# Two attentions on one core: the transposes of a group alternate with products of the matrix fill instead of standing in a row

## Chip, cores and metric

The kernel runs on one core of one Trainium2 chip. The metric is device time in microseconds (us) of one execution, the median of the runs shown. A profiled execution of its own gives the span and the trace.

## The reference, cut to what matters

Two transformer blocks run over 1024 tokens of width 1024, in float32. Each block has an attention, and each attention needs transposes of its weights of attention:

```python
# block 1: sliding window, 8 heads, blocks of 128 queries, 256 keys each
scores = einsum('bnqhgd,bnkhd->bnhgqk', qb, keys) * scale      # masked to the band
probs = softmax(concat([scores, sink]))[..., :-1]
out = einsum('bnhgqk,bnkhd->bnqhgd', probs, vals)
# block 2: stick breaking, 8 heads, blocks of 128 queries, all earlier keys
z = einsum('bhqd,bhkd->bhqk', qb, k) * scale
between = cumsum(log_sigmoid(-z), reverse) - log_sigmoid(-z)
out = einsum('bhqk,bhkd->bhqd', exp(log_sigmoid(z) + between), v)
# block 2: differential, 4 heads
out = (softmax(q1 @ k1.T) - lam * softmax(q2 @ k2.T)) @ v
```

Around them stand projections of 1024 x 1024 tokens by some thousand columns each. Those of w_in, w_in_2 and w_gate_2 bear on the change.

## The kernel before, in words

Every float32 product is made of three TensorE matmuls of rounded halves (high by high, high by low, low by high), each with a 128x128 weight and 512 moving columns. One such matmul is called a product below, and a run of 24 of them fills one accumulation bank.

Two classes carry the order of the work. `Fill` (line 115) is a generator of projections: each step of `run` (line 134) issues one product at line 152, calls `tick`, which runs the callbacks that are due (evacuations of a finished bank four products after its last one, stores, later parts of a norm), calls `units.ahead()`, which may issue the rounding of the next weight unit (high half at line 101, low half at line 102) and the load of the one two further on, and yields. `Plan` (line 163) holds the attention's steps by tick and slot. `Plan.run` (line 172) writes out by hand the order of TensorE (PE), ScalarE (ACT), VectorE (DVE) and GpSimd (POOL): in every tick it goes through the slots; at a slot with a name it issues the steps put there, at a slot with a number it draws products from the fill until `due(t, slot)` have been given in all. The count is cumulative, so that what was given early is not given again.

In **block 1** (`attention`, line 799) a tile of 128 queries has two groups of heads with one or two key blocks: 30 groups of four transposes in all. In a tick the slots are A, B, B2, 0, E, D0, D, F, C, F2, 1, G, H. `turn` (line 849, slot D) issues the group's four transposes at line 852 into a bank called `tp`; `halves` (slot F, line 857) copies it on ACT, `low` (slot F2, line 861) subtracts on DVE, and `pv` (slot D0 of the next tick, lines 265 to 267) multiplies the result with the values. Slot 1 lies after F2.

In **block 2** the slots are load, A, A2, B, B2, C0, C, 0, D0, D, F, 1, G. There are 96 units of stick breaking (12 a head) and 48 units of the differential attention, each with one to four key blocks of 128, and so one to four transposes, made by `transposed` (line 1732, the transposes at line 1735). For a stick unit the scores are in slot B (lines 1723 to 1729), `weigh` in slot A of the next tick (ACT lines 1813 to 1815, DVE lines 1816 to 1825), `final` in A2 (line 1828), the transposes (`mid`) in slot G, the last of tick t+2, the split of their bank (`end`, lines 296 and 297) in slot C of t+3 and `pv` (line 1836) in slot D0 of t+4. For a differential unit the transposes are in slot D, `end` in slot F of the same tick, and `pv` (line 1976) in slot G of the next. Eight more groups of four turn the finished differential output (line 1921). The last user of `transposed` is `diff_qk` (line 1676): 16 groups of four, called by the fill's own callbacks.

There are two `tp` banks, two `mm` banks for the fill, three `sc` banks for scores and one `po` bank. SyncE (SP) issues the loads and stores, in the order in which the program comes to them.

Of the kernel before, what the change touches and what calls it, by code (L numbers as in the profile page):

```python
# [114 lines left out]
class Fill:  # L115
# [18 lines left out]
    def run(self):  # L134

        kern, units = self.kern, self.units
        for kind, half, tt, us, free, out in self.products:
            ps = kern.ps("mm")
            ah, al = kern.actH[half], kern.actL[half]
            for k in range(KT):  # L140
                if kind == "n":
                    wh, wl = (w[:, k * P : k * P + P] for w in units.get(us[0]))
                    xh, xl = ah[:, k, :], al[:, k, :]
                    steps = ((wh, xh), (wh, xl), (wl, xh))
                else:
                    c = slice((k % 2) * HALF, (k % 2) * HALF + HALF)
                    wh, wl = (w[:, c] for w in units.get(us[k // 2]))
                    s = slice(tt * P, tt * P + P)
                    xh, xl = ah[:, k, s], al[:, k, s]
                    steps = ((xh, wh), (xh, wl), (xl, wh))  # L150
                for i, (l, r) in enumerate(steps):
                    kern.last_mm = kern.nc.tensor.matmul(ps, l, r, start=k == 0 and i == 0, stop=k == KT - 1 and i == 2)  # L152
                    self.tick()
                    if i == 2 and free and (k == KT - 1 if kind == "n" else k % 2 == 1):
                        self.after(6 if kind == "t" else 2, units.free)
                    units.ahead()
                    yield
            self.after(LAG, lambda out=out, ps=ps: out(ps))
        while self.late:
            self.tick()  # L160


class Plan:
# [8 lines left out]
    def run(self, ticks, slots, fill, due, lead=0):  # L172

        E = mybir.EngineType
        steps = fill.run()
        given = 0
        with self.tc.manual_schedule(engines={E.PE, E.Activation, E.DVE, E.Pool}):
            for t in range(ticks):
                while given < lead:
                    next(steps, None)  # L180
                    given += 1
                for slot in slots:
                    if isinstance(slot, int):
                        while given < due(t, slot):
                            next(steps, None)
                            given += 1
                    else:
                        for fn in self.ev.pop((t, slot), ()):
                            fn()
            for _ in steps:  # L190
                pass
        assert not self.ev and not fill.late, (self.ev, fill.late)


class Kern:
# [311 lines left out]
    def block1_mix(self, stack):  # L507
# [287 lines left out]
        plan = Plan(self.tc)  # L795
# [3 lines left out]
        def attention(t):  # L799
# [49 lines left out]
            def turn(g, b):  # L849
                pt = A["pt"] = self.ps("tp")  # L850
                for j in range(4):
                    nc.tensor.transpose(pt[:, j * P : j * P + P], A[g * 4 + j][:, b * P : b * P + P], self.ident)

            def halves(g, b):
                h = self.t(pl, [P, HALF], "pth", bufs=2, dt=F32R)
                A["hl"] = h, self.t(pl, [P, HALF], "ptl", bufs=2, dt=F32R)
                nc.scalar.copy(h, A["pt"])
# [38 lines left out]
            for g in range(2):  # L896
                for b in range(nb):
                    u = t0 + 5 + g * 2 + b
                    at(u, "D", lambda g=g, b=b: turn(g, b))
                    at(u, "F", lambda g=g, b=b: halves(g, b))  # L900
                    at(u, "F2", low)
                    at(u + 1, "D0", lambda g=g, b=b: pv(g, b))
                at(u + 1, "F", lambda g=g: out(g))
# [67 lines left out]
        for t in range(NT):  # L971
            attention(t)
# [624 lines left out]
    def block2_attn(self, stack):  # L1597
# [45 lines left out]
        def diff_qk(which):  # L1643
# [31 lines left out]
            def turn(t, qn):  # L1675
                pt = transposed(qn.rearrange("p h d -> p (h d)"), 4)
                fill[0].after(3, lambda: store(t, pt))
# [54 lines left out]
        def transposed(src, nb):  # L1732
            pt = self.ps("tp")
            for i in range(nb):
                nc.tensor.transpose(pt[:, i * P : i * P + P], src[:, i * P : i * P + P], self.ident)  # L1735
            return pt

        def cut(L):
# [9 lines left out]
        plan = Plan(self.tc)  # L1748
# [3 lines left out]
        def paired(d, key, w):  # L1752


            def mid():
                d["pt"] = transposed(d[key], w // P)

            def end():
                hl = d["hl"] = self.t(pl, [P, 4, 2, P], "phl", bufs=3, dt=F32R)[:, : w // P]
                self.split(hl[:, :, 0, :], hl[:, :, 1, :], d["pt"][:, :w].rearrange("p (a b) -> p a b", b=P))  # L1760

            return mid, end
# [117 lines left out]
        def diff_tile(H, h, qt, chunks, L):  # L1880
# [39 lines left out]
            def turn():  # L1920
                Q["pt"] = transposed(Q["o4"].rearrange("p a b -> p (a b)"), 4)
# [94 lines left out]
        n = len(ticks)  # L2016
# [332 lines left out]
```

## Time and profile before

| what | us |
|---|---|
| median of the runs shown | 2677.01 (2676.76 to 2686.59) |
| profiled execution, its own time | 2672.5 |
| its span, first to last instruction | 2670.7 |
| PE busy | 2597.1 (97% of the span) |
| weight loads of PE (PEld) busy | 2085.7 (78%) |
| DVE, ACT, POOL busy | 1870.3, 1158.2, 660.9 (70%, 43%, 25%) |

The first attention with its fill lies at 113 to 345 us of the span, the second at 1129 to 1830 us. PE's matmuls are pipelined and their ends are modelled, so durations overlap: what an instruction costs on PE is read from the distance between starts, not from its duration. PEld rows are the loads of the 128x128 weights that stand before each matmul. A number in square brackets behind a row is idle time of that engine before it, with what ended it.

### The profile page before, as it was taken

How to read it: one execution, taken by the hardware profiler on the slowest of the kernel's cores; microseconds unless marked ns; L12 is line 12 of the kernel's file. 1: busy time of each engine (PE TensorE's matmuls, PEld its weight loads, DVE VectorE, ACT ScalarE, POOL GpSimd, SP SyncE). 2: the span in 40 equal slices, each digit the busy share in tenths (PEclk: the TensorE clock that was granted, in tenths of full speed). 3: DMA queues.
4: the chain of work that ended last, by engine and by line, in shares of the span. 5: the costliest groups of instructions: out<-in, count | busy, mean ns of one | idle time of the engine just before them, and what ended most of it. 6: DMA issues, size and time to landing. Idle time of an engine off the chain costs nothing. (4 is left out here: it accounts for less than half of the span.)

```text
span 2670.7 us, 34280 instructions
## 1 busy us (share of the span) xinstructions
PE 2597.1 (97%) x12078; PEld 2085.7 (78%) x12078; DVE 1870.3 (70%) x2836; ACT 1158.2 (43%) x2080; POOL 660.9 (25%) x571
## 2 busy tenths in 40 slices
PE   9999999999999999899999999999999999999999
PEld 8766787788778778677777777787887788887887
DVE  5688867887887566726788777775636767776654
ACT  3444525433333334526766765554316222323442
POOL 4323254002343332311255111110001003331501
PEclk8999999999999999999999999999999999999999
DMA  6243575434555886346344343336634446565973
GB/s 257 80 158 123 162 264 193 175 137 169 200 171 192 301 285 216 126 128 198 92 131 126 123 132 116 112 105 230 240 142 144 158 140 209 171 215 189 369 243 133
DMA packets 224604, 470.84 MB, mean 176 GB/s; under 512 B 26672, under 2 KB 73904, under 8 KB 224432
## 3 DMA queue, kind: packets, MB, share of 16 engines
q1 hardware_dynamic: 224432, 468.65, 52.3%
q8 instruction: 95, 1.56, 0.2%
q14 instruction: 77, 0.63, 0.1%
HBM read 331.18 MB, written 137.36 MB: 175 GB/s over the span
## 5 line engine op out<-in xcount | busy, mean ns | idle before, releaser
L1353 POOL TENSOR_TENSOR raw<-raw,raw 128x512 f32<-128x512 f32 x78 | 141.3, 1811 | 417.0 <-DMA raw<-in_w_down 210.8
L152 PE MATMUL mm<-ah,wh 128*128 128x512 f32 x544 | 219.8, 404 | 1.8 <-DVE gb L606 1.8
L152 PE MATMUL mm<-ah,wl 128*128 128x512 f32 x544 | 219.3, 403 | 0.0
L152 PE MATMUL mm<-al,wh 128*128 128x512 f32 x544 | 219.0, 403 | 0.0
L102 POOL TENSOR_TENSOR wl<-raw,wh 128x1024 fp32r<-128x1024 f32 x44 | 106.5, 2421 | 399.3 <-DVE wh L101 159.8
L1216 DVE TENSOR_TENSOR W<-W 128x1024 f32<-128x1024 f32 x132 | 129.9, 987 | 14.5 <-DMA W<-in_w_up 12.5
L152 PEld LDWEIGHTS mm<-ah,wh 128*128 128x128 f32 x544 | 102.6, 189 | 22.5 <-issue 2.6
L152 PEld LDWEIGHTS mm<-ah,wl 128*128 128x128 f32 x544 | 102.6, 189 | 20.7 <-issue 2.5
L152 PEld LDWEIGHTS mm<-al,wh 128*128 128x128 f32 x544 | 102.7, 189 | 20.1 <-issue 2.2
L152 PE MATMUL mm<-wl,ah 128*128 128x512 f32 x256 | 102.4, 400 | 1.0 <-DVE wl L102 0.8
L152 PE MATMUL mm<-wh,al 128*128 128x512 f32 x256 | 103.2, 403 | 0.0
L152 PE MATMUL mm<-wh,ah 128*128 128x512 f32 x256 | 102.3, 400 | 0.0
L1152 PE MATMUL sc<-s,wh 128*128 128x512 f32 x344 | 100.6, 394 | 1.6 <-DVE u L1288 1.5
L1820 DVE TENSOR_TENSOR_SCAN w<-sc,w,w 128x383 f32<-128x383 f32 (+3 forms) x96 | 97.4, 1015 | 3.4
L297 DVE TENSOR_TENSOR wl<-rb,wh 128x1024 fp32r<-128x1024 f32 x52 | 77.1, 1483 | 23.7 <-ACT wh L296 19.4
L1507 PE MATMUL sc<-wh,ah 128*128 128x512 f32 x272 | 91.2, 389 | 0.0
L297 DVE TENSOR_TENSOR phl<-tp,phl 128x512 fp32r<-128x512 f32 (+2 forms) x144 | 78.3, 544 | 15.6 <-ACT phl L296 15.5
L1152 PE MATMUL mm<-ah,wh 128*128 128x512 f32 x236 | 79.7, 400 | 8.8 <-DVE wt L1105 5.0
L1816 DVE SCALAR_TENSOR_TENSOR w<-sc,w 128x384 f32<-128x384 f32 (+3 forms) x96 | 53.2, 554 | 45.7 <-ACT w L1815 45.4
L296 ACT CAST phl<-tp 128x512 fp32r<-128x512 f32 (+2 forms) x144 | 67.9, 472 | 34.5 <-PE tp L1735 34.2
L244 POOL TENSOR_SCALAR rs<-ss 128x1 f32<-128x1 f32 x40 | 16.5, 413 | 264.4 <-ACT xn L312 243.3
L1152 PE MATMUL mm<-al,wh 128*128 128x512 f32 x236 | 77.9, 399 | 3.9 <-ACT s L1172 3.9
(561 smaller groups left out, 7603.9 us busy)
## 6 DMA issues: line engine op xcount, KB each, us to landing
W<-in_w_up SPq DMA_DIRECT2D x88, 512.0 KB, 4.5
adaw<-in_ada_w SPq DMA_DIRECT2D x64, 256.0 KB, 3.0
raw<-in_w_in SPq DMA_DIRECT2D x31, 512.0 KB, 3.7
Fa<-g SPq DMA_DIRECT2D x44, 256.0 KB, 2.6
Fb<-g SPq DMA_DIRECT2D x44, 256.0 KB, 2.9
tw<-in_w_down SPq DMA_DIRECT2D x20, 512.0 KB, 5.3
rb<-in_w_down SPq DMA_DIRECT2D x40, 256.0 KB, 5.3
raw<-Fa SPq DMA_DIRECT2D x18, 512.0 KB, 4.9
```

Source lines behind the costliest of these rows:

```text
L102: (nc.vector if i in self.vec else nc.gpsimd).tensor_tensor(out=wl, in0=raw, in1=wh.bitcast(F32), op=ALU.subtract)
L152: kern.last_mm = kern.nc.tensor.matmul(ps, l, r, start=k == 0 and i == 0, stop=k == KT - 1 and i == 2)
L244: self.nc.gpsimd.tensor_scalar(out=out, in0=ss, scalar1=1.0 / n, scalar2=EPS, op0=ALU.mult, op1=ALU.add)
L296: nc.scalar.copy(h, src)
L297: nc.vector.tensor_tensor(out=l, in0=src, in1=h.bitcast(F32), op=ALU.subtract)
L1152: self.last_mm = nc.tensor.matmul(ps, l, r, start=first and k == 0 and i == 0, stop=last and k == 3 and i == 2, skip_group_check=True)
L1216: sub = lambda out, x, y: nc.vector.tensor_tensor(out=out, in0=x, in1=y, op=ALU.subtract)
L1353: eng.tensor_tensor(out=q[out], in0=q[x], in1=q[y], op=op)
L1507: self.last_mm = nc.tensor.matmul(bank, l, r, start=opens and i == 0 and j == 0, stop=closes and i == n - 1 and j == 2, skip_group_check=True)
L1816: nc.vector.scalar_tensor_tensor(out=ls, in0=z, scalar=0.0, in1=ls, op0=ALU.min, op1=ALU.subtract)
L1820: nc.vector.tensor_tensor_scan(out=sg[:, : w - 1][:, ::-1], data0=z[:, 1:w][:, ::-1], data1=ls[:, : w - 1][:, ::-1], initial=sg[:, w - 1 : ...
```

## The change

After every transpose of `turn` and `transposed` a new function of the plan, `one`, draws one product from the fill. It does so only when the plan's lead has been given and when the fill is not running already, so that a group issued from one of the fill's callbacks draws nothing. The product counts as given. The loops that draw up to a number become `more(n)`, which sets and clears the flag.

```diff
         given = 0
+        running = False
+
+        def one():
+
+            nonlocal given, running
+            if given >= lead and not running:
+                running = True
+                next(steps, None)
+                running = False
+                given += 1
+
+        def more(n):
+            nonlocal given, running
+            running = True
+            while given < n:
+                next(steps, None)
+                given += 1
+            running = False
+
+        self.one = one
...
-                while given < lead:
-                    next(steps, None)
-                    given += 1
+                more(lead)
                 for slot in slots:
                     if isinstance(slot, int):
-                        while given < due(t, slot):
-                            next(steps, None)
-                            given += 1
+                        more(due(t, slot))
...
                     nc.tensor.transpose(pt[:, j * P : j * P + P], A[g * 4 + j][:, b * P : b * P + P], self.ident)
+                    plan.one()
...
                 nc.tensor.transpose(pt[:, i * P : i * P + P], src[:, i * P : i * P + P], self.ident)
+                plan.one()
```

## Rows read from the trace of the kernel before

**Rows 1.** Windows of both attentions: busy us (x instructions) PE, PEld, DVE, ACT, POOL; clock; DMA.
```profile
113.00:345.00 232.00, 221.70 (x1123) 165.58 (x1122) 183.69 (x432) 108.55 (x254) 68.01 (x51) 0.99 0.49 155
1129.00:1830.00 701.00, 687.82 (x3486) 538.54 (x3485) 497.95 (x1052) 403.96 (x976) 156.49 (x187) 1.00 0.42 126
```

**Rows 2.** Groups of PE, both attentions: count | busy us, mean ns | idle before, releaser.
```profile
L1735 PE MATMUL tp<-cons,w 128*128 128x128 f32 x432 | 70.8, 273 | 3.5 <-DVE phl L297 3.5
...
L1735 PE MATMUL tp<-cons,do 128*128 128x128 f32 x32 | 4.8, 272 | 0.0
...
L852 PE MATMUL tp<-cons,prob 128*128 128x128 f32 x120 | 18.6, 276 | 0.2 <-DVE prob L847 0.2
```

**Rows 3.** Timeline of PE, a group of four: start us, us, engine, line, tiles, count.
```profile
1643.38 0.39 PE L152 MATMUL mm<-al,wh 128*128 128x512 f32 x1
1643.61 0.60 PE L1735 MATMUL tp<-cons,w 128*128 128x128 f32 x4
...
1644.29 0.39 PE L152 MATMUL mm<-ah,wh 128*128 128x512 f32 x1
```

**Rows 4.** Timeline of PE and PEld, a transpose alone between products.
```profile
1649.07 0.39 PE L152 MATMUL mm<-ah,wl 128*128 128x512 f32 x1
1649.30 0.27 PE L1735 MATMUL tp<-cons,w 128*128 128x128 f32 x1
...
1649.64 0.40 PE L152 MATMUL mm<-al,wh 128*128 128x512 f32 x1
...
1650.10 0.39 PE L152 MATMUL mm<-ah,wh 128*128 128x512 f32 x1
...
1649.30 0.19 PEld L152 LDWEIGHTS mm<-ah,wh 128*128 128x128 f32 x1
```

**Rows 5.** Timeline of PE, eight matmuls of one column each.
```profile
230.85 0.95 PE L379 MATMUL tp<-cons,ada 128*128 128x1 f32 x8
231.66 0.43 PE L265 MATMUL po<-pth,vh 128*64 128x512 f32 x1
```

**Rows 6.** Timeline of PE around equal scores: behind a product, behind two transposes.
```profile
1156.81 0.40 PE L152 MATMUL mm<-wl,ah 128*128 128x512 f32 x1
...
1157.73 0.45 PE L152 MATMUL mm<-wh,al 128*128 128x512 f32 x1
...
1216.49 0.39 PE L152 MATMUL mm<-ah,wh 128*128 128x512 f32 x1
...
1217.63 0.45 PE L152 MATMUL mm<-al,wh 128*128 128x512 f32 x1
```

**Rows 7.** Timeline of a group of block 1 and its readers.
```profile
309.93 0.63 PE L852 MATMUL tp<-cons,prob 128*128 128x128 f32 x4
...
311.21 0.69 DVE L861 TENSOR_TENSOR ptl<-tp,pth 128x512 fp32r<-128x512 f32 x1 [0.95 <-ACT pth L857]
...
313.63 0.40 PE L266 MATMUL po<-ptl,vh 128*64 128x512 f32 x1
```

**Rows 8.** Timeline of a stick unit, from its scores to its transposes.
```profile
1284.29 0.33 PE L1729 MATMUL sc<-r_stm,r_ident 128*128 128x128 f32 x1
...
1284.76 0.60 ACT L1813 ACTIVATE w<-sc 128x512 f32<-128x512 f32 x1
...
1286.59 0.62 ACT L1828 ACTIVATE w<-w 128x512 f32<-128x512 f32 x1
...
1287.62 0.49 PE L1735 MATMUL tp<-cons,w 128*128 128x128 f32 x3
```

**Rows 9.** Groups of DVE, block 1: part of an evacuation of the fill.
```profile
L603 DVE SCALAR_TENSOR_TENSOR gb<-u,cols,gb 128x512 f32<-128x512 f32 x12 | 10.6, 884 | 1.3 <-ACT gb L601 1.0
```

**Rows 10.** Waits of PE in both attentions: us in total, times, longest us.
```profile
PE tp L1735 <- DVE phl L297: 3.5, 4, 1.4
PE po L1836 <- DVE phl L297: 2.1, 2, 1.6
...
PE po L266 <- DVE ptl L861: 3.3, 5, 1.3
```

## Prediction

> **What bounds the kernel now.** I first read the windows over the two attentions [rows 1]. PE is busy for 221.7 of 232 us in the first and 687.8 of 701 us in the second, at a granted clock of 0.99 and 1.00 of full speed, that is the upper of its two levels, 2.4 GHz. Next come DVE with 184 of 232 and 498 of 701 us. So PE sets the time of both stretches, and all that the change can win or lose is PE time: what a transpose costs, and the 10.3 + 13.2 = 23.5 us in which PE has nothing to run.
>
> Then I counted [rows 2]: 432 transposes for the weights of attention in block 2, 32 for the differential output, 120 in block 1, together 584. By the code they stand in 144 + 8 + 30 = 182 groups. The change puts a product between neighbours at 584 - 182 = 402 places. The product drawn behind a group's last transpose stands where the next work of PE stood before. Durations are of no use here, since matmuls overlap (273 ns a transpose by its mean); the distances of starts in the timeline of PE are.
>
> A group of four [rows 3]: from the product at 1643.38 to the one at 1644.29 lie 0.91 us, which hold two products and four transposes. A transpose alone [rows 4]: from 1649.07 to 1649.64 lie 0.57 us with two products and one transpose; the next two products take 1650.10 - 1649.64 = 0.46 us, 0.23 each. So four in a row cost 0.91 - 0.46 = 0.45 us, 0.11 each, and one between two products costs 0.57 - 0.46 = 0.11 us. That is the reading on which the prediction rests: **the price is the same in both places.**
>
> Why it should be so is seen from two rows. Eight matmuls of a single moving column each need 231.66 - 230.85 = 0.81 us [rows 5], 0.10 apiece, so between short matmuls it is the next weight load that sets the pace, not the columns. And behind the lone transpose the load of the product's weights starts at 1649.30, with the transpose's own start [rows 4], and not earlier: it can't hide in the product before, because there the transpose's load stands. In a row each transpose waits for its own load, and at the end the product waits for its load: four exposed loads for four transposes. Alternating, each transpose's load hides behind a product, and each product's load behind a transpose of 0.11 us is exposed instead: four again.
>
> **The change, part by part.**
>
> *402 places where a product now separates two transposes.* One switch to a transpose and back costs 0.11 us with the transpose itself in it [rows 4], as does each in a row [rows 3]. 402 x (0.11 - 0.11) = 0 us. No row shows two such switches within one product's time, so the price is bounded from both sides. Below, the transpose could vanish behind the products: -0.11 us each, 402 x 0.11 = -44 us. Above, the product's load could be laid bare in full, 0.19 us [rows 4] in place of 0.11: 402 x 0.08 = +32 us. I take 0, since rows 4 hold both switches and are the nearest by far: nothing in an alternation differs from them but what stands two matmuls away.
>
> The Trainium skill, TensorE: Matmul & The Clock Gate (Back-to-back issue gap), gives 134 cycles for a matmul of 128 columns at the full clock, 56 ns as an estimate. By that figure a transpose whose load is hidden would cost 0.056 instead of 0.11 us and the sum would be 402 x 0.054 = 22 us lower; the lone transpose of rows 4 has its load hidden and costs 0.11, so the trace disagrees.
>
> *The product behind a group's last transpose.* In 96 stick units the next work of PE is the scores of slot B. The same scores of 256 columns take from product to product 1157.73 - 1156.81 = 0.92 us behind a product and 1217.63 - 1216.49 = 1.14 us behind two transposes [rows 6]: a difference of 0.22, twice 0.11. So what follows a group does not matter either: 0 us.
>
> *What the products take with them.* Each drawn product runs the callbacks that are due. These move earlier by up to four products in the order of ACT, DVE and POOL, and the stores and weight loads among them pass up to one tick's loads of queries and keys in SP's order. No work is added. The count is cumulative, so the slot behind draws as many fewer, and the fill ends with the same number of products. POOL is busy for 157 of 701 us [rows 1] and has room. What SP loads is wanted some ticks later: I cost it at nothing, and where that cover fails, PE waits for weights or queries at a transfer's lateness. Weight by weight, the load, its rounding and its product keep their order.
>
> *What gets late.* A group of four now takes three products longer: its last transpose comes 3 x 0.23 = 0.69 us later, and so does the copy by ACT and the subtraction by DVE where these wait for it. In block 1 a group's low half is ready at 311.21 + 0.69 = 311.90 and the matmul that reads it starts at 313.63 [rows 7], 1.7 us later. Of this 0.69 goes: covered, and 1.0 us is left. But an evacuation that now stands ahead of `low` can take this too: two of the multiplications of a convolution alone are 2 x 0.884 = 1.77 us of DVE [rows 9]. Of the 624 products of the first fill (26 outputs of 24) 120 are drawn in groups, 19%, so some 5 of 26 evacuations move ahead of their group's split; each may overrun the slack by 0.69 + 1.77 - 1.7, up to 0.8 us, and I take 0.4 us: +2 us. In block 2 the fill has 74 outputs and the distance from a group to `pv` is a whole tick or more. In the second place the scores of a stick unit come up to four products (0.92 us) later against its own transposes. In the tightest unit that I found the scores' last matmul starts at 1284.29, ACT reads them at 1284.76, its last exponential ends at 1286.59 + 0.62 = 1287.21 and the transposes follow at 1287.62 [rows 8]: 0.41 us to spare. Here the group between is of three, so the scores come 0.69 later; ACT had 0.1 us of margin behind them, the chain slips by 0.6 and the transposes wait 0.2 us. It is the tightest that I found; I count such slips at under 0.5 us in all, and let them go into the rounding.
>
> The waits for a late split are now 3.5 + 2.1 + 3.3 = 8.9 us [rows 10]. Below: all of them vanish by a luckier order, -9 us. Above: each of block 1's 30 groups loses 0.5 us, the middle between nothing and a bit over the 0.8 above, +15 us.
>
> **Sum.** 0 + 0 + 2 us on the profiled execution of 2672.5 gives 2674.5. The median of the runs is 4.5 us above that execution, so the forecast is 2679 us, 0.1% from the median. About 0.5%, 13 us, is what a measurement of this kernel can tell from no change.
>
> **Rivals.**
>
> *The loads hide (faster).* If PE loaded two weights ahead, a transpose between products would cost less than in a row. With all of it hidden the time is 2679 - 44 = 2635 us, with half of it 2657. (By the Trainium skill's figure, quoted above, the half is what would come.) For it speaks that the load of a transpose indeed begins with the product before [rows 3, 4]; against it that the lone transpose has this already and still costs 0.11 us. Chance 0.05.
>
> *Alternating lays the product's load bare (slower).* The place is the first matmul behind each inner transpose, the price 0.19 - 0.11 = 0.08 us, and it decides from the second switch on, when the next load must wait until the transpose's weights have been left. 402 x 0.08 = 32 us, 2711 us. The rows for a lone transpose show no such loss over two products, but none shows the pair repeated. Chance 0.05.
>
> *The split comes too late (slower).* The cover of `pv` and of the stick chain is used up, by the 0.69 us together with evacuations that moved forward. It decides when some 20 groups lose 0.7 us each, 14 us: 2693 us. For it: DVE has 48 us of room in 232 in block 1 and the waits of rows 10 show groups with no slack; against it: where ACT or DVE is the late one already, a later transpose changes nothing, and most groups keep over 1 us. Chance 0.05, of which 0.04 lies beyond 0.5%.
>
> *The change does nothing.* If the guard kept `one` from drawing, or the fill had run out, the order would be the old one: 2677 us. The guard does so for the 16 groups that come from the fill's callbacks, no others, and the products reach to the end of the attention. It is inside the forecast's range.
>
> **How the numbers follow.** The forecast (with the last rival in it) has 0.85. Faster by over 0.5%: 0.05. Slower by over 0.5%: 0.05 + 0.04 = 0.09. Within: 0.86. The range takes in the bounds of the stalls against the 2677 us of now, -9 and +15 us: 2668 to 2692 us. It leaves the two rivals of the loads outside, with 1 in 10 between them.
>
> **What the next profile would show.** Right: in the timeline of PE a transpose and a product alternate with 0.34 us from transpose to transpose (0.23 + 0.11), 1.36 us for four pairs, against 0.45 + 0.92 = 1.37 before; the busy time of DVE and ACT is the same; idle time of PE over both attentions is 20 to 30 us. Wrong: pairs at 0.29 us or less (the loads hide), at 0.42 us (they are laid bare), or PE waits of over 15 us more at lines 266, 1836 and 1976, or a granted clock under 0.99 in a stretch of groups. Should the scores of stick units show idle time of ACT in front of line 1813 that grows by more than 0.9 us a unit, the term for what gets late is too small.

## The result, and the profile after

The changed kernel takes 2698.31 us (median of 7 runs, 2690.65 to 2704.49) against 2679.70 us before in the same comparison: a ratio of 1.0059, 95% interval 1.0044 to 1.0075. The medians lie 18.6 us apart; the ratio is not the quotient of the medians and stands for some 16 us. No measurable change was forecast, and the time lies 6 us above the range. The profiled execution took 2700.85 us, its span is 2699.1 us.

The windows over both attentions, each from the first to the last product of its fill (columns as in [rows 1]), first of the kernel before, cut the same way:

```profile
113.50:343.30 229.80, 219.50 (x1113) 163.74 (x1112) 181.85 (x429) 106.80 (x252) 65.81 (x51) 0.99 0.48 154
1129.10:1824.70 695.60, 682.42 (x3463) 534.12 (x3462) 495.11 (x1049) 399.44 (x970) 156.49 (x187) 1.00 0.41 125
```

and of the changed kernel:

```profile
117.10:355.50 238.40, 221.75 (x1113) 162.14 (x1112) 183.32 (x429) 107.11 (x252) 65.85 (x51) 0.99 0.46 147
1145.80:1851.30 705.50, 690.04 (x3462) 525.28 (x3461) 494.82 (x1049) 401.98 (x970) 159.02 (x187) 0.99 0.41 123
```

The instructions are the same. The first attention is 8.6 us longer, and PE idles for 238.40 - 221.75 = 16.6 us of it instead of 10.3. The second is 9.9 us longer, with 15.5 us idle instead of 13.2 and a lower clock, so that PE's busy time grew too. The other 10 us of the spans' difference lie ahead of, between and behind the attentions, where nothing was edited. I don't explain them: over the profiles of this study these stretches take 112.3 to 117.1, 784.3 to 790.3 and 843.3 to 850.5 us, in no order with the edits. That the two attentions alone (18.5 us) make about the 18.6 us between the medians is chance: against a second profile of the kernel before (the control below) they are 13.1 us longer, 10.6 us of it idle time of PE.

The alternation itself is as forecast. PE's timeline in the changed kernel, a group of four (columns as in [rows 3], which it answers to):

```profile
1669.85 0.27 PE L1752 MATMUL tp<-cons,w 128*128 128x128 f32 x1
1669.88 0.48 PE L152 MATMUL mm<-ah,wl 128*128 128x512 f32 x1
1670.19 0.27 PE L1752 MATMUL tp<-cons,w 128*128 128x128 f32 x1
1670.22 0.48 PE L152 MATMUL mm<-ah,wh 128*128 128x512 f32 x1
1670.54 0.27 PE L1752 MATMUL tp<-cons,w 128*128 128x128 f32 x1
```

From transpose to transpose lie 0.34 and 0.35 us, 0.23 for the product and 0.11 to 0.12 for the transpose, the price in a row. The starts of a pair differ by 0.03 us only, but the sum of the two is what it was.

What grew are waits. PE's waits in the changed kernel, first attention and then second (line, total us, times, longest us; compare [rows 10]; lines 282, 1752 and 1854 were 266, 1735 and 1836):

```profile
PE po L282 <- DVE ptl L878: 6.6, 7, 1.5
PE po L281 <- ACT pth L874: 3.1, 2, 2.0
...
PE tp L1752 <- DVE phl L313: 7.6, 5, 3.8
...
PE po L1854 <- DVE phl L313: 1.2, 2, 0.7
```

Line 282 waits for the low half of block 1's weights 6.6 instead of 3.3 us, line 281 for the high half 3.1 instead of 0.6 us, and transposes in block 2 wait for a free bank, that is for the split at line 313, 7.6 instead of 3.5 us. Of the 7.6, one wait of 3.79 us is that of `diff_qk`'s transposes, which did not wait before; the transposes of the weights wait 3.8 us, about as long as before.

**The largest stall of the first attention.** The changed kernel's timeline from a group's last transpose to its value products:

```profile
300.62 0.27 PE L868 MATMUL tp<-cons,prob 128*128 128x128 f32 x1
...
302.58 0.71 ACT L617 ACTIVATE gb<-u,cols 128x512 f32<-128x512 f32 x1
303.33 1.54 DVE L619 SCALAR_TENSOR_TENSOR gb<-u,cols,gb 128x512 f32<-128x512 f32 x2 [1.43 <-ACT gb L617]
304.90 0.75 DVE L622 SCALAR_TENSOR_TENSOR gb<-mm,cols,gb 128x512 f32<-128x512 f32 x1
305.69 0.63 ACT L626 ACTIVATE gb<-gb 128x512 f32<-128x512 f32 x1 [2.40 <-DVE gb L622]
305.97 2.15 DVE L863 TENSOR_SCALAR prob<-prob,den 128x256 f32<-128x256 f32 x4
306.23 0.57 ACT L874 CAST pth<-tp 128x512 fp32r<-128x512 f32 x1
306.85 0.45 PE L281 MATMUL po<-pth,vh 128*64 128x512 f32 x1 [2.02 <-ACT pth L874]
308.05 0.68 DVE L878 TENSOR_TENSOR ptl<-tp,pth 128x512 fp32r<-128x512 f32 x1
308.78 0.69 PE L282 MATMUL po<-ptl,vh 128*64 128x512 f32 x1 [1.49 <-DVE ptl L878]
```

The transposes are done at 301, but ACT copies the bank (line 874) only at 306.23. ACT first has exponentials until 302.58. Then comes, still ahead of the copy, a convolution's finish, which goes from ACT to DVE and back to ACT (lines 617 to 626): ACT idles for 2.40 us inside it, though the copy behind had all that it needed. The Trainium skill, PSUM — Partial Sum Buffer (Engine vs sequencer instructions), says that the queues of ScalarE and VectorE are strict first-in first-out; the row at 305.69 agrees. The second wait, 1.49 us, has DVE ahead of it: the scaling of attention weights (line 863, slot C) starts only behind the finish, at 305.97, and takes 2.15 us, where the kernel before takes 1.14; why it is slower here is not shown. In the kernel before the same finish of the same place comes behind the copy (then line 857), and PE waits for nothing:

```profile
294.82 0.56 ACT L857 CAST pth<-tp 128x512 fp32r<-128x512 f32 x1
295.29 0.72 ACT L601 ACTIVATE gb<-u,cols 128x512 f32<-128x512 f32 x1
...
296.82 0.68 DVE L861 TENSOR_TENSOR ptl<-tp,pth 128x512 fp32r<-128x512 f32 x1
297.42 1.53 DVE L603 SCALAR_TENSOR_TENSOR gb<-u,cols,gb 128x512 f32<-128x512 f32 x2
298.49 0.39 PE L266 MATMUL po<-ptl,vh 128*64 128x512 f32 x1
```

**The largest stall of the second attention.** The changed kernel's timeline:

```profile
1480.78 0.69 DVE L101 CAST wh<-raw 128x1024 fp32r<-128x1024 f32 x1 [1.82 <-DMA raw<-in_w_in2t]
1481.51 1.23 DVE L102 TENSOR_TENSOR wl<-raw,wh 128x1024 fp32r<-128x1024 f32 x1
...
1484.75 0.40 DVE L313 TENSOR_TENSOR phl<-tp,phl 128x256 fp32r<-128x256 f32 x1
1485.21 1.12 PE L1752 MATMUL tp<-cons,dqn 128*128 128x128 f32 x4 [3.79 <-DVE phl L313]
```

DVE waits 1.82 us for the load of a weight unit, with its rounding (lines 101, 102) at the head of the queue; behind the rounding comes the next unit's scan (lines 1834 to 1838, 1482.65 to 1484.84), and only then the split that frees a bank of transposes. PE stands for 3.79 us. This is the largest wait, but by the experiments below the loss does not come and go with it.

With both stalls the granted clock falls. Windows of the changed kernel (columns as in [rows 1]), up to the first stall and behind it, and from inside the second (PE idles until 1485.21):

```profile
301.00:307.00 6.00, 3.98 (x19) 2.31 (x17) 4.43 (x11) 3.60 (x12) 0.60 (x1) 1.00 0.57 179
308.00:314.50 6.50, 5.72 (x19) 3.80 (x20) 4.49 (x15) 2.46 (x7) 1.11 (x2) 0.50 0.14 40
...
1482.00:1488.50 6.50, 3.29 (x10) 2.32 (x11) 5.54 (x11) 1.11 (x2) 4.75 (x7) 0.50 0.77 267
```

0.50 is the lower level, 1.2 GHz. PE runs at half speed where it has work again, and so a stall costs more than its idle time.

### The profile page after: what moved, and what is told of

Same layout as the page of the kernel before. It is cut to its first block, busy times and chain, and to the rows that moved or that the text cites. A ratio compares the mean times of both kernels' runs of the same rounds, so it can differ in the third digit from the quotient of the medians.

```text
span 2699.1 us, 34278 instructions
## 1 busy us (share of the span) xinstructions
PE 2615.1 (97%) x12078; PEld 2082.0 (77%) x12078; DVE 1875.0 (69%) x2836; ACT 1161.3 (43%) x2080; POOL 656.9 (24%) x571
## 5 line engine op out<-in xcount | busy, mean ns | idle before, releaser
L152 PE MATMUL mm<-ah,wh 128*128 128x512 f32 x544 | 229.2, 421 | 2.3 <-DVE gb L622 2.3
L152 PE MATMUL mm<-ah,wl 128*128 128x512 f32 x544 | 229.0, 421 | 0.0
L152 PE MATMUL mm<-al,wh 128*128 128x512 f32 x544 | 228.9, 421 | 0.0
L1752 PE MATMUL tp<-cons,w 128*128 128x128 f32 x432 | 117.6, 272 | 3.8 <-DVE phl L313 3.8
L152 PE MATMUL mm<-wl,ah 128*128 128x512 f32 x256 | 108.4, 424 | 2.1 <-POOL wl L102 2.1
L152 PE MATMUL mm<-wh,al 128*128 128x512 f32 x256 | 109.2, 427 | 0.0
L152 PE MATMUL mm<-wh,ah 128*128 128x512 f32 x256 | 108.2, 423 | 0.0
L1169 PE MATMUL mm<-ah,wh 128*128 128x512 f32 x236 | 80.0, 402 | 9.7 <-DVE wt L1122 6.0
L1169 PE MATMUL mm<-al,wh 128*128 128x512 f32 x236 | 78.1, 400 | 3.8 <-ACT s L1189 3.8
```

The lines of the kernel that those rows point to most:

```text
L1169: self.last_mm = nc.tensor.matmul(ps, l, r, start=first and k == 0 and i == 0, stop=last and k == 3 and i == 2, skip_group_check=True)
```

## Experiments

Ratios are against the kernel before, run beside each kernel on the same chip.

**The two attentions apart.** The first keeps `plan.one()` in `turn` alone, the second in `transposed` alone.

```diff
 # first only: in transposed
-                plan.one()
 # second only: in turn
-                    plan.one()
```

> Alternation in the first attention only (30 groups). Theory, order and bank: the change costs PE stalls in both attentions, because the drawn products carry their evacuations and weight roundings ahead of the group's own split, and because the last transpose is late; then this run keeps the 8.7 us that the first attention lost in the profile and none of the second's 9.9: 2686 to 2690 us, first attention 238 us long, second 696. Rival, the clock alone (a general loss of granted clock by the alternating stream): the first attention's share is 90 of 402 places, 4 us, 2684 us, with no more idle time of PE than before.

> Alternation in the second attention only (152 groups). Theory: first attention at 230 us as before, second at 703 to 706, 2688 to 2692 us, with waits of PE at the transposes on the split of the group before (line 1752) and drops of the granted clock behind them. Rival, chance: the second attention's loss was three drops of the clock that fall by luck; then its length comes back to 696 to 699 us and the time to 2680 to 2684.

First only: 2690.20 us, 1.0032 (1.0019 to 1.0045). Second only: 2688.02 us, 1.0026 (1.0011 to 1.0041). 0.32% + 0.26% = 0.58%, as much as the whole change in its first comparison (0.59%; its repeat below gave 0.40%). Windows of the edited attention, first of the one and then of the other kernel:

```profile
116.80:355.20 238.40, 221.79 (x1113) 162.19 (x1112) 183.26 (x429) 107.07 (x252) 65.79 (x51) 0.99 0.44 146
```

```profile
1131.10:1836.40 705.30, 690.04 (x3463) 525.39 (x3461) 494.59 (x1049) 401.70 (x970) 158.76 (x187) 0.99 0.40 123
```

They repeat the lengths and idle times of the changed kernel to 0.3 us. Each attention pays for itself. By length alone one profile would not show this: the second attention, unedited, took 699.2 us in the kernel with the first only, and 704.0 us in the one with the subtraction moved in the first attention (below), against 695.6 us in the first profile of before. Its idle time keeps the two apart: 11.3 to 13.2 us in every profile with that attention unedited, 14.3 to 16.7 us in every one with the alternation and its callbacks.

**The transposes in a row again, the products directly behind them.** This leaves the early draw and takes the alternation away.

```diff
                 for j in range(4):
                     nc.tensor.transpose(pt[:, j * P : j * P + P], A[g * 4 + j][:, b * P : b * P + P], self.ident)
+                for j in range(4):
                     plan.one()
...
                 nc.tensor.transpose(pt[:, i * P : i * P + P], src[:, i * P : i * P + P], self.ident)
+            for i in range(nb):
                 plan.one()
```

> Both attentions; the transposes of a group stand in a row as before, and the same number of products is drawn directly behind the group's last one. So the callbacks of the products move as in the changed kernel, the last transpose is as early as before. Theory, moved callbacks: as slow as the changed kernel, 2694 to 2702 us, idle time of PE in the first attention near 16 us. Rival, the late last transpose: back to 2680 us, first attention 230 us.

2688.01 us, 1.0029 (1.0016 to 1.0042): half of the loss or more stays with no alternation in it; the time lies between the two expectations. Its windows:

```profile
114.40:346.90 232.50, 221.59 (x1112) 164.81 (x1111) 181.75 (x429) 106.98 (x252) 65.28 (x51) 0.99 0.45 152
1132.90:1836.90 704.00, 688.54 (x3462) 531.72 (x3461) 495.11 (x1049) 400.19 (x970) 157.92 (x187) 0.99 0.40 124
```

PE's idle time falls to 10.9 us in the first attention, and stays at 15.5 in the second.

**The alternation without what products call.** Drawn products run no callbacks and no roundings; what is owed is paid with the next product of a numbered slot.

```diff
+    def pay(self):
+        while self.owed and not self.quiet:
+            self.owed -= 1
+            self.tick()
+            self.units.ahead()
...
-                    self.tick()
+                    self.owed += 1
+                    self.pay()
...
-                    units.ahead()
+                    if not self.quiet:
+                        units.ahead()
...
-                running = True
+                running = fill.quiet = True
```

> The changed kernel, but a product drawn in a group runs no callbacks and rounds no weights; they are run behind the next product that is drawn outside a group. The transposes alternate and the last one is late as in the change, the callbacks stand behind the group's split, as before. Theory, moved callbacks: 2680 to 2684 us. Rival, the late last transpose: 2694 to 2700 us.

2687.83 us, 1.0024 (1.0010 to 1.0038). Better than the change, but no return to before: PE idles for 12.5 us in the first attention and 13.9 in the second. It lies between what was expected of either theory. By the code, what is owed is paid in one burst, roundings and the freeing of units among it, and the last transpose is still late; which of these keeps the loss is not told apart by this run.

**The changed kernel again, and whose wait it is.** In block 2 the wait of 3.8 us is that of `diff_qk`'s own transposes (rows above: `dqn`) for a bank, so one theory was that too many groups want the two banks. The second kernel lets no such group come out of a drawn product.

```diff
-        for x in [x for x in self.late if x[0] <= self.clock]:
+        for x in [x for x in self.late if x[0] <= self.clock and not (self.quiet and x[1] in self.held)]:
...
-                fill[0].after(TURN_LAG, lambda: turn(t, qn))
+                later = lambda: turn(t, qn)
+                fill[0].held.add(later)
+                fill[0].after(TURN_LAG, later)
```

> The changed kernel once more, beside the others and on their chip. If the two attentions add up (e1 +0.32%, e2 +0.26%): +0.5 to +0.65%, 2694 to 2699 us; its profile with the same lengths of the two attentions as before, 238 and 705 us, within 3 us. If they don't add, 2688 to 2692.

> The changed kernel, but the fill's own transposes (16 groups of the query and key norms) are not issued between or directly behind the transposes of a group of the plan: when they fall due in a group they wait for the next product outside of one. Theory, two transpose banks: the wait of 3.8 us at the fill's transposes on the split of the group before goes down to under 1.5 us, the second attention from 705 to 701 us or less, its idle time from 15.5 to 11 to 13 us, time 3 to 6 us under the changed kernel. Rival, DVE's backlog whatever the bank: the wait moves to the next reader of the split, the length stays at 704 to 706.

Again: 2693.55 us, 1.0040 (1.0021 to 1.0058). Its profile has the first attention at 238.0 us with 14.6 us idle and the second at 705.3 us with 15.4. Turn held out: 2693.41 us, 1.0044 (1.0030 to 1.0057), the same. PE's groups of instructions in its second attention (columns as in [rows 2]):

```profile
L1755 PE MATMUL tp<-cons,w 128*128 128x128 f32 x432 | 118.0, 273 | 3.8 <-DVE phl L314 3.8
L1755 PE MATMUL tp<-cons,dqn 128*128 128x128 f32 x64 | 10.1, 282 | 2.6 <-DVE phl L314 2.6
```

The wait did not move to another user of the bank: `diff_qk`'s transposes (`dqn`) still stand, 2.6 us instead of 3.8, and those of the weights wait 3.8 us as in the change. Neither the fall to under 1.5 us that the theory asked for nor the move that its rival expected came, and the second attention is no shorter (706.1 us). So keeping these groups out of drawn products does not mend it; what PE waits for is still DVE's split.

**The subtraction ahead of slot C in block 1**, in the kernel before and in the changed one. If the place of `low` in DVE's order were the cause, this would mend it.

```diff
-... "F", "C", "F2", 1, "G", "H")
+... "F", "F2", "C", 1, "G", "H")
```

> The kernel before with one edit: in the first attention the split's subtraction (slot F2) is issued on DVE ahead of the scaling of the weights (slot C). Theory, a late split is what stalls PE at the value matmuls: their 4.4 us of waits fall to 1 to 2 us, the first attention from 230 to 225 to 227 us, time 2674 to 2678. Rival, DVE's throughput: what is moved back delays the transposes in their turn, the length stays within 1 us.

> The changed kernel with the same one edit. Theory: its waits at the value matmuls (9.7 us in the profile) fall by 4 to 6 us, the first attention from 238 to 232 to 234 us, the time 4 to 7 us under the changed kernel. Where an evacuation holds ACT in front of the split's copy the wait stays, so not all goes. Rival as in the run without the change: within 1 us of 238.

On the kernel before 2686.06 us, 1.0011 (0.9998 to 1.0025); on the changed one 2701.65 us, 1.0058 (1.0039 to 1.0077), no better than the change itself. PE's waits in the first attention of the former:

```profile
PE sc L815 <- DVE rm L823: 3.1, 3, 1.7
PE sc L815 <- DVE ql L300: 1.7, 1, 1.7
...
PE po L266 <- DVE ptl L861: 0.6, 2, 0.3
```

The wait of line 266 shrank from 3.3 to 0.6 us, and scores wait for DVE at line 815 instead; the idle time of the first attention is 11.0 us, against 10.3 before. `low` is not wrongly placed by itself; here moving one part of DVE's work handed the wait to the next. In the changed kernel the first attention took 243.5 us, with 15.7 us idle at a clock of 0.96.

**Callbacks or roundings, with a control.** The control is the kernel before once more. One kernel takes only the roundings out of the drawn products, the other only the callbacks (but those that free a weight unit).

```diff
 # roundings out: where a product of the fill is issued
-                    units.ahead()
+                    if not self.quiet:
+                        units.ahead()
 # callbacks out: in tick
-        for x in [x for x in self.late if x[0] <= self.clock]:
+        for x in [x for x in self.late if x[0] <= self.clock and (not self.quiet or x[1] == self.units.free)]:
...
 # both: in one
-                running = True
+                running = fill.quiet = True
```

> The kernel before, once more, for a second profile of it. If its first profile (granted clock 0.999 in the second attention) was a lucky one, as the lengths of the unchanged second attention in other runs say (699 and 704 us): first attention 228 to 233 us, second 697 to 704 us at a clock of 0.984 to 0.995, with the same 13 us of idle time of PE. Rival, the first profile is typical: second attention 694 to 697 us, clock 0.997 or more.

> The changed kernel, but a product drawn in a group does not call for the rounding of the next weight unit; its other callbacks run as in the change. Theory for the second attention: a rounding that waits on DVE for its load stands ahead of the next unit's scan and split; without it the wait of 3.8 us goes, idle time of PE there from 15.5 to 13 or 14 us, length 698 to 702 us; the first attention stays at 237 to 239 us; time 2685 to 2691. Rival, the evacuations: the second attention stays at 15 us idle and 704 to 706 us, time 2692 to 2697.

> The complement: a product drawn in a group calls for roundings as in the change, but runs no other callbacks (evacuations, later parts of norms, the fill's own transposes) than the freeing of a unit. Theory: the first attention, whose evacuations of a convolution hold ACT and DVE ahead of the split, goes from 238 to 232 to 235 us with 11 to 13 us idle; the second keeps its waits, 15 us idle, 702 to 706 us; time 2687 to 2692. Rival, roundings in the first attention as well: 237 to 239 us.

The control took 2677.73 us in its single run. Roundings out: 2692.03 us, 1.0044 (1.0029 to 1.0059), no gain beside the change, though the largest stall of the second attention is gone from it:

```profile
L1754 PE MATMUL tp<-cons,dqn 128*128 128x128 f32 x64 | 9.6, 273 | 0.0
```

The stall of `dqn` is thus made by roundings that are called early: it stands in every kernel here whose drawn products call them in the second attention, and in no other. But the transposes of the weights now wait 4.9 us, and the idle time is 16.2 and 15.3 us, as in the change.

Callbacks out: 2683.30 us, 1.0009 (0.9997 to 1.0022): most of the loss is gone. Windows of the control, and of the kernel with the callbacks out:

```profile
113.40:344.60 231.20, 220.95 (x1112) 164.98 (x1111) 181.80 (x429) 106.72 (x252) 65.91 (x51) 0.99 0.46 153
1129.80:1829.40 699.60, 688.30 (x3462) 538.85 (x3461) 494.80 (x1049) 399.65 (x970) 156.41 (x187) 0.99 0.40 124
```

```profile
115.10:346.50 231.40, 218.94 (x1112) 160.65 (x1111) 181.72 (x429) 107.12 (x252) 66.56 (x51) 1.00 0.45 150
1133.10:1833.20 700.10, 688.20 (x3462) 524.90 (x3461) 494.66 (x1049) 402.94 (x970) 156.30 (x187) 0.99 0.40 124
```

With the callbacks held both attentions are as long as in the control, the second too, which I had expected to keep its waits. Its timeline at the place of the first stall has the copy (now line 875) ahead of the finish again, and PE waits for nothing there:

```profile
297.74 0.57 ACT L875 CAST pth<-tp 128x512 fp32r<-128x512 f32 x1
298.21 0.73 ACT L618 ACTIVATE gb<-u,cols 128x512 f32<-128x512 f32 x1
...
299.34 0.68 DVE L879 TENSOR_TENSOR ptl<-tp,pth 128x512 fp32r<-128x512 f32 x1
...
300.08 0.44 PE L283 MATMUL po<-ptl,vh 128*64 128x512 f32 x1
```

The stall of `dqn`, whose roundings still run, stays almost as long as in the change (PE's groups in the second attention):

```profile
L1753 PE MATMUL tp<-cons,w 128*128 128x128 f32 x432 | 117.8, 273 | 1.5 <-DVE phl L314 1.5
L1753 PE MATMUL tp<-cons,dqn 128*128 128x128 f32 x64 | 10.1, 282 | 3.4 <-DVE phl L314 3.4
```

So the second attention is as short as the control's with this stall in it, and no faster kernel came of taking the stall away. What shrank is the wait of the weights' transposes, 1.5 instead of 3.8 us.

This kernel holds its callbacks until the next numbered slot, as the one that held callbacks and roundings did (1.0024, 1.0010 to 1.0038). The two intervals overlap, so the runs don't tell them apart.

The control also shows that the first profile of before was fortunate: its second attention took 695.6 us, the control's 699.6 with less idle time (11.3 against 13.2 us) and a lower clock.

**The fourth corner, and a kernel made from the finding.** The row with the callbacks held combines the two edits above. For the other, the kernel before gets the reverse of what hurt: in the numbered slot whose work stands ahead of a group and so ahead of its split (0 in block 1, 1 in block 2, ahead of the stick units' slot G) no roundings are called; they come with the other numbered slot, which lies behind the split. A last one holds the other callbacks there as well.

```diff
                     if isinstance(slot, int):
+                        fill.quiet = slot == hush
...
-                    units.ahead()
+                    if not self.quiet:
+                        units.ahead()
...
-        plan.run(40, ("A", "B", "B2", 0, "E", "D0", "D", "F", "C", "F2", 1, "G", "H"), fill, due, 100)
+        plan.run(40, ("A", "B", "B2", 0, "E", "D0", "D", "F", "C", "F2", 1, "G", "H"), fill, due, 100, 0)
```

> Transposes in a row, the same number of products drawn directly behind them, and these products run no callbacks but the freeing of a unit. It differs from the run with callbacks out (+0.09%) only in that the transposes do not alternate with the products. If alternation and the later last transpose cost what is left there: -0.05 to +0.05% against the kernel before, 2680 to 2683 us, first attention 229 to 231 us. If they cost nothing: +0.05 to +0.15%, 2683 to 2686 us, as with callbacks out.

> The kernel before, transposes in a row, with roundings called for only behind a group's split: not in slot 0 of the first attention and not in slot 1 of the second. If roundings ahead of scans and splits are what stalls PE in the kernel before too, its idle time of 23.5 us in both attentions falls to 17 to 20 and the time to 2674 to 2679 us, 0.1 to 0.2% under the kernel before. Rival, DVE is full there and an order only moves the wait: within 0.1% of it.

> The kernel before with roundings and all other callbacks (but the freeing of a unit) called for only behind a group's split. Theory, callbacks ahead of a split stall PE in the kernel before as well: waits at the value matmuls of the first attention (3.9 us before) under 1.5 us, 2 to 4 us under the run with roundings behind alone: 2674 to 2677. Rival, held callbacks bunch up behind the split and hold the next scans and scores: 2680 to 2684 us.

Row with callbacks held: 2677.50 us, 0.9987 (0.9972 to 1.0001), below both ranges expected. The stall of `dqn` is in it as well (3.5 us). Roundings behind the split: 2678.73 us, 0.9984 (0.9972 to 0.9996), the lowest ratio here, though by 0.16% only, and not told apart from the row with callbacks held. Its idle time, 7.8 + 13.3 us, is that of the control (21.6 us), so the profile does not show where a gain would come from. All callbacks behind the split: 2684.12 us, 1.0018 (1.0005 to 1.0032): the idle time of the second attention grows to 17.2 us. That callbacks held so long come in a bunch and delay what follows is my reading of it, as it was the rival expected. Windows of the row with callbacks held, and of the roundings behind the split:

```profile
115.30:345.20 229.90, 221.44 (x1113) 165.23 (x1112) 181.57 (x429) 106.90 (x252) 65.89 (x51) 0.99 0.46 154
1135.10:1833.20 698.10, 687.20 (x3463) 532.17 (x3462) 495.00 (x1049) 401.33 (x970) 156.35 (x187) 0.99 0.40 125
```

```profile
112.50:340.00 227.50, 219.66 (x1112) 164.76 (x1111) 178.51 (x429) 106.84 (x252) 65.39 (x51) 0.98 0.46 156
1130.00:1830.80 700.80, 687.53 (x3462) 539.17 (x3461) 493.46 (x1049) 399.75 (x970) 156.28 (x187) 0.99 0.40 124
```

The four corners, ratio against before (95%) and PE's idle us in the first and second attention, each by the windows (callbacks without the roundings, which run in all four; the changed kernel stands in the last cell with both of its comparisons and profiles):

| | callbacks held | callbacks run |
|---|---|---|
| in a row, products behind | 0.9987 (0.9972 to 1.0001); 8.5, 10.9 | 1.0029 (1.0016 to 1.0042); 10.9, 15.5 |
| alternating | 1.0009 (0.9997 to 1.0022); 12.5, 11.9 | 1.0059 (1.0044 to 1.0075), 1.0040 (1.0021 to 1.0058); 16.6, 15.5 and 14.6, 15.4 |

Down a column and along a row: the callbacks that drawn products run cost some 0.4% (11 us) in a row and 0.3 to 0.5% alternating, the alternation some 0.2% (6 us) with the callbacks held, 0.1 to 0.3% with the callbacks run. The first is shown: in a row the two intervals lie apart, alternating they lie apart for the first comparison and touch for the second. The second is likely only: its intervals overlap but for one of the two comparisons of the change, and its idle time lies almost all in the first attention (8.5 to 12.5, 10.9 to 14.6 or 16.6 us). There it is larger than what the callbacks add (2.4 us in a row, 2.1 to 4.1 alternating); in the second attention the callbacks add 4.6 and 3.6 us, the alternation up to 1.0.

## Why the prediction was wrong

**The price of the alternation (right).** 0.11 us a transpose, 0.34 a pair, in place of the 0.45 us for four that stand in [rows 3]. Neither rival of the loads came true. The Trainium skill's figure by which half of it would hide (TensorE: Matmul & The Clock Gate, Back-to-back issue gap; 0.056 us as an estimate) is not what the timeline shows: 0.34 - 0.23 is 0.11. The kernels that alternate and that don't, both with callbacks held, agree with it over the whole attentions: PE is busy for 907.1 and 908.6 us.

**Nothing for what follows a group (right).** The row with its products directly behind, callbacks held, is not slower than before (0.9987), though nearly every group is followed by something else.

**"What the products take with them", at nothing (wrong).** I looked at it for SP's order and for POOL's room, where it is indeed small, and left ACT's and DVE's order to the next term. The callbacks are the larger part of the loss, some 11 us in a row and 8 to 13 us alternating.

**"What gets late", +2 us (wrong, the failed step).** The mechanism was the right one in block 1, in place and kind: an evacuation now stands ahead of a group's split. Its size was off in three ways. First, I priced an evacuation at two DVE multiplications, 1.77 us [rows 9]. The convolution's finish is a chain over two engines, on the timeline above from 302.58 to the copy's start at 306.23, 3.65 us, and the copy waits for all of it, idle time of ACT included. Second, I counted lost slack group by group, against a typical 1.7 us [rows 7]. The waits come from few groups that lose far more, 2.02 + 1.49 us in one place of block 1.

Third, I gave block 2 less than 0.5 us because the distance from a group to its readers is a tick. But the late split also keeps the bank, and the next transposes wait for that: 7.6 us against 3.5. The growth is the one stall of `dqn`, and a rounding makes it, not an evacuation; yet the loss does not go with it, since two kernels with that stall are as fast as before (0.9987, 1.0009) and the one that lost it alone is not (1.0044). What goes with the callbacks in block 2 is smaller and spread out, 2.3 of 3.6 us of it at the weights' transposes.

Measured, PE's idle time in both attentions was 32.1 and 30.0 us in the two profiles of the change, 23.5 and 21.6 us in the two of before: 6.5 to 10.6 us more, where the sum had 2 and the forecast 20 to 30 us in all. The rest is busy time of PE, which no term of mine held, though I had named a lower clock among the signs of a wrong forecast: 9.9 us of the attentions' 18.5 against the fortunate first profile with its higher clock, 2.5 us of 13.1 against the control. The signs that I had named for too small a term did not show: PE's waits at the value products grew by far less than 15 us, and ACT's idle time ahead of the stick units' first exponential went from 8.6 to 12.3 us over 96 units, far from 0.9 us a unit. I had counted on many groups each a little late, and a few were very late.

**The rival.** "The split comes too late" gave 2693 us, and the two comparisons gave 2698 and 2694. Its price, 0.7 us for each of some 20 groups, gave nearly the right sum in the wrong shape: few groups lose much. Against it I held that where ACT or DVE is late already, a later transpose changes nothing. That holds for the transposes, but the callbacks make ACT and DVE themselves later (3.65 us at the first stall). A chance of 0.05 was too low.

**What is not settled.** That the alternation's share is the later last transpose (0.69 us) fits PE's idle time in the first attention but was not tried apart from it. Why the kernel that holds callbacks and roundings alike is still slower than before (1.0024) is open, and so are the shares of single callbacks.

## What to carry to other kernels

When a change draws fill work earlier, list what each drawn step issues on every engine, and follow its longest chain across engines: an evacuation that went from ACT to DVE and back held up the work queued behind it on ACT for its whole length, here 3.65 us, 2.40 of them idle. Then look for the work that is queued behind it and for who holds a bank meanwhile. Here products drawn behind a group and ahead of its split cost nothing without their callbacks (0.9987), and 0.4% more with them; in the kernel before, callbacks held back altogether until behind the split cost 0.2% (1.0018). And don't take the longest stall of a profile for the cause: here one stall of 3.4 us and more stood in kernels with no loss, and a kernel without it was no faster.

## What the runs showed of the hardware

In the changed kernel the granted clock stood at 0.50 for the 6.5 us of two windows: from inside the second of two PE waits of 2.02 and 1.49 us (window at 308), and from inside a wait of 3.79 us (window at 1482). Waits need not bring this: the first profile of before had waits of up to 2.4 us in its second attention, 13.2 us in all, and a clock of 1.00 over the whole of it; the control had 11.3 us at 0.99, and the same code took 695.6 and 699.6 us. One kernel's runs spread with the clock: over 35 runs of the kernel before the shortest took 2672.72 us at a mean granted clock of 0.990, the longest 2690.17 us at 0.984. A dozen runs of a kernel beside 23 to 35 of before gave intervals of 0.12 to 0.15% to either side, so a difference of 0.2% asks for about as many and can't be read from one profile.
